# Differential attention on one Trainium2 core: the first head's split written nine units later, behind the parts of the values' third weight

## The chip, the cores and the metric

The kernel runs on one core of a Trainium2 chip. The metric is the time on the device in microseconds (us), as the median of several runs. The engines are TensorE (PE in the profile, PEld for its weight loads), VectorE (DVE), ScalarE (ACT), GpSimd (POOL) and SyncE (SP). Here SP issues the loads of weights, and POOL issues the copies between places in on-chip memory that this change moves.

## The reference

A trunk of four layers over 512 tokens of width 1024. Each layer is a mixer and a gated feed-forward block, both behind a root-mean-square norm. The mixers are S5, gated linear attention, differential attention, and S5 again. The change lies in the third layer's mixer:

```python
def diff_attn_mixer(h, positions, w_qkv, lam_q1, lam_k1, lam_q2, lam_k2, subln_g, w_o, lambda_init):
    q, k, v = jnp.split(h @ w_qkv, 3, axis=-1)
    q = partial_rope(q.reshape(bsz, seq, 2 * DIFF_HEADS, DIFF_HD), positions) * DIFF_HD ** -0.5
    k = partial_rope(k.reshape(bsz, seq, 2 * DIFF_HEADS, DIFF_HD), positions)
    v = v.astype(f32).reshape(bsz, seq, DIFF_HEADS, 2 * DIFF_HD)
    lam = (jnp.exp(jnp.sum(lam_q1 * lam_k1)) - jnp.exp(jnp.sum(lam_q2 * lam_k2)) + lambda_init)
    ...
        s = jnp.einsum('bqhd,bkhd->bhqk', qb, k)
        mask = chunk_id[:, None, None, :] <= qcid[:, None, :, None]
        p = jax.nn.softmax(jnp.where(mask, s, NEG_INF), axis=-1)
        p = p.reshape(bsz, DIFF_HEADS, 2, Q_BLOCK, seq)
        a = p[:, :, 0] - lam * p[:, :, 1]
        return jnp.einsum('bhqk,bkhd->bqhd', a, v)
    ...
    o = o * lax.rsqrt(jnp.mean(o * o, axis=-1, keepdims=True) + 1e-5) * subln_g
    o = o * (1.0 - lambda_init)
    return o.reshape(bsz, seq, D_MODEL) @ w_o
```

There are eight heads, each with two queries and two keys of 64 channels and one value of 128. A head's output is the difference of two softmaxes, applied to the values.

## The kernel before

**Precision by parts.** A float32 operand of a large matmul is split in two: a high part, which ACT makes by a cast (`high`, L346), and a low part, the remainder, which DVE makes by a subtraction (`low`, L350). A product is then three matmuls: high by high, high by low, low by high (`mm3`, lines 370 to 372). The method `last` keeps the newest instruction of each kind: `self.last["high"]` is the newest cast of a weight and `self.last["low"]` the newest remainder.

**Weights.** A weight arrives in blocks of 256 rows by 512 columns, 512 KB. SP loads a block into one of three staging buffers (`staged`, L336, tag `wst`); the parts go to one of five buffers of the tag `whl`. A buffer is claimed anew when its earlier tenant has been read for the last time.

**Units.** `gemm_units` multiplies the 512 tokens by 512 columns of a weight as a generator. Over the 1024 rows of the weight it takes four blocks in turn; a block has two slices of 128 rows, and each slice meets four tiles of 128 tokens. One unit is one slice and one tile, that is, one `mm3`; a block makes eight units and a projection 32. The block's load and split are written when its first unit is asked for. At the last slice each tile is evacuated.

**Projections.** `project(hf, z)` does this for half `hf` of the heads, with z = 0 for the queries, 1 for the keys, 2 for the values. For queries and keys the evacuation scales by the norm's factor (ACT, L2143), applies the rotation on DVE (lines 2148 to 2154), and puts the transposition of the tile into a list that is worked off six units later (`turn`: four transposes on PE, L2159, and a copy on ACT, L2160). So the keys' four tiles are turned within the first units of the values. The values are evacuated on ACT (L2165).

**The head's split.** `prepare(j)` readies head j for its scores. It casts the head's queries and keys (ACT, L2179), takes the remainder (DVE, L2180), both into a tile `hl`, and copies the parts by eight DMAs on POOL's queue (L2187 and L2188) into `qs` and `ks`, so that high and low parts lie in the two halves of the partitions. `hl` has one buffer of its own for most heads, `qs` has two, and `ks` claims one of the five buffers `whl` that the weights use too. For head 1, `hl` also claims a `whl` buffer. `scores(i)` multiplies them (PE, L2205) for tile i mod 4 of head i div 4.

**Order.** PE's instructions run in the order in which they are written. Those of the other engines, and the claims of buffers, are put in order by the compiler's scheduler, which prefers what is written first among what is ready in its own model of the time. `issue_after(x)` adds, to each instruction written in its block on the engine of x, an edge that keeps it behind x in that engine's order. It adds no semaphore.

**The sequence at the change.** Queries of the first four heads, the tables, keys, then eight units of the values; the list of turns is emptied; head 0 is prepared; the values' other 24 units follow. Then the projections of the other four heads begin, and after two of their units come the scores of head 0's first tile. The attention loop over 32 tiles runs on between the remaining units, with `prepare(j + 1)` at each head's first tile.

## Time and profile before

| | |
|---|---|
| median of 3 runs | 2325.21 us (2324.91 to 2325.57) |
| the profiled execution | 2320.61 us |
| its span, from the first to the last instruction | 2318.9 us |
| mean granted clock of TensorE | 0.989 |
| PE busy from 1250 to 1290 us | 38.51 of 40.00 us |
| PE busy from 1380 to 1440 us | 53.79 of 60.00 us |

The profile shows one execution. Busy time is summed per engine; matmuls are pipelined, so that a matmul's own length overlaps the next one's start, and the distance of two starts says more than a length. In a row of the order of time the columns are the start and the length in us, the engine, the line, the operation, output and inputs with their shapes, a count, and in brackets the idle time of that engine just before and what ended it. A row with a count above one merges neighbours. The queries' projection ends and the keys' begins near 1199.6 us of the span; the attention ends near 1460 us.

### The profile page before, as it was taken

The page shows a single profiled execution, that of the slowest core. Times are in us where ns is not written, and L with a number is a line of the kernel's source. Part 1 is how long each engine was busy: PE and PEld are TensorE (multiplying, and loading weights), DVE is VectorE, ACT ScalarE, POOL GpSimd, SP SyncE. Part 2 cuts the span into 40 slices and gives each one's busy share as a digit, 9 for nine tenths or more (in the row PEclk, how much of TensorE's full clock was granted, in tenths as well). Part 3 has the DMA queues.
Part 4 walks back from the last instruction along what each step waited for, and adds up shares of the span by engine and source line. Part 5 has one row for each costly group of instructions (what it writes and reads, how often), then busy time and mean ns, then how long its engine had stood idle before and what let it go on. Part 6 is the DMA issues. An engine that isn't in the chain of part 4 may idle for free. (4 is left out here: it accounts for less than half of the span.)

```text
span 2318.9 us, 37158 instructions
## 1 busy us (share of the span) xinstructions
PE 2221.3 (96%) x14847; PEld 1969.5 (85%) x14847; DVE 1593.3 (69%) x2461; ACT 1112.6 (48%) x1769; POOL 284.5 (12%) x394
## 2 busy tenths in 40 slices
PE   5899999999999999999999999999999899999997
PEld 3788979898877789898988887899999788989996
DVE  8784877786624578776744675976766965967674
ACT  5533645454453355555535675654534224635342
POOL 1000141522000010101002131110000100101000
PEclk8999999999999999999999999999999999999999
DMA  4156567663422457575336365876641555766531
GB/s 85 37 141 171 138 166 183 169 175 97 129 73 73 133 138 196 155 191 156 100 124 151 91 150 143 216 206 152 171 96 46 140 158 151 191 161 161 160 81 64
DMA packets 293927, 319.91 MB, mean 138 GB/s; under 512 B 70077, under 2 KB 233177, under 8 KB 293498
## 3 DMA queue, kind: packets, MB, share of 16 engines
q1 hardware_dynamic: 231130, 235.79, 33.9%
q0 software_dynamic: 62624, 81.75, 19.1%
q8 instruction: 117, 1.92, 0.3%
q14 instruction: 56, 0.46, 0.1%
HBM read 285.62 MB, written 16.65 MB: 130 GB/s over the span
## 5 line engine op out<-in xcount | busy, mean ns | idle before, releaser
L350 DVE TENSOR_TENSOR whl<-wst,whl 128x1024 fp32r<-128x1024 f32 x272 | 331.9, 1223 | 280.6 <-ACT whl L346 279.8
L346 ACT CAST whl<-wst 128x1024 fp32r<-128x1024 f32 x272 | 285.6, 1052 | 382.8 <-PE acc L372 259.8
L535 PE MATMUL a<-side,whl 128*128 128x256 f32 x3168 | 384.9, 278 | 10.0 <-ACT whl L346 5.9
L535 PEld LDWEIGHTS a<-side,whl 128*128 128x128 f32 x3168 | 371.7, 189 | 12.5 <-ACT whl L346 7.2
L370 PE MATMUL acc<-whl,act 128*128 128x512 f32 x704 | 278.0, 395 | 1.2 <-DVE g L580 0.8
L371 PE MATMUL acc<-whl,act 128*128 128x512 f32 x704 | 274.9, 391 | 0.0
L372 PE MATMUL acc<-whl,act 128*128 128x512 f32 x704 | 274.7, 390 | 0.0
L535 PE MATMUL c<-side,whl 128*128 128x256 f32 x2112 | 255.6, 277 | 5.8 <-DVE whl L350 5.8
L535 PEld LDWEIGHTS c<-side,whl 128*128 128x128 f32 x2112 | 248.1, 189 | 6.6 <-DVE whl L350 6.6
L350 DVE TENSOR_TENSOR whl<-slot,whl 128x1024 fp32r<-128x1024 f32 x105 | 127.9, 1223 | 65.7 <-ACT whl L346 65.1
L370 PEld LDWEIGHTS acc<-whl,act 128*128 128x128 f32 x704 | 132.1, 188 | 30.8 <-DVE g L580 1.2
L372 PEld LDWEIGHTS acc<-whl,act 128*128 128x128 f32 x704 | 132.2, 188 | 27.8
L371 PEld LDWEIGHTS acc<-whl,act 128*128 128x128 f32 x704 | 132.2, 188 | 26.0 <-issue 0.2
L346 ACT CAST whl<-slot 128x1024 fp32r<-128x1024 f32 x105 | 110.1, 1054 | 73.9 <-PE acc L372 28.1
L370 PE MATMUL acc<-whl,hT 128*128 128x512 f32 x352 | 142.9, 406 | 2.1 <-DVE ro L2151 1.5
L371 PE MATMUL acc<-whl,hT 128*128 128x512 f32 x352 | 137.9, 392 | 1.0 <-DVE whl L350 1.0
L372 PE MATMUL acc<-whl,hT 128*128 128x512 f32 x352 | 137.9, 392 | 0.0
L535 PE MATMUL a<-sides,whl 128*128 128x256 f32 x1056 | 134.0, 283 | 1.6 <-DVE x L518 1.6
L535 PE MATMUL d<-sides,whl 128*128 128x256 f32 x1056 | 133.4, 283 | 1.3 <-ACT whl L346 1.3
L535 PEld LDWEIGHTS a<-sides,whl 128*128 128x128 f32 x1056 | 129.5, 191 | 2.7 <-issue 2.0
L535 PEld LDWEIGHTS d<-sides,whl 128*128 128x128 f32 x1056 | 128.9, 191 | 1.9 <-ACT whl L346 1.9
L571 POOL DMA_DIRECT2D wst<-in_ffn_w_gate_up_dram x44 | 57.1, 1297 | 436.5 <-DMA wst<-in_ffn_w_gate_up_dram 239.1
(449 smaller groups left out, 3909.1 us busy)
## 6 DMA issues: line engine op xcount, KB each, us to landing
wst<-in_ffn_w_gate_up_dram SPq DMA_DIRECT2D x88, 512.0 KB, 4.7
wst<-in_ffn_w_down_dram SPq DMA_DIRECT2D x88, 512.0 KB, 4.5
slot<-in_ffn_w_gate_up_dram SPq DMA_DIRECT2D x69, 512.0 KB, 5.5
wst<-in_ffn_w_gate_up_dram POOLq DMA_DIRECT2D x44, 512.0 KB, 6.2
halves<-in_ffn_w_gate_up_dram SPq DMA_DIRECT2D x42, 512.0 KB, 5.7
wst<-in_s_w_glu_dram SPq DMA_DIRECT2D x32, 512.0 KB, 4.5
wst<-in_gla_w_in_dram SPq DMA_DIRECT2D x24, 512.0 KB, 3.7
wst<-in_diff_w_qkv_dram SPq DMA_DIRECT2D x24, 512.0 KB, 3.7
```

What stands on the lines that cost most here:

```text
L346: self.last["high"] = self.nc.scalar.copy(hl[:, 0], w[:])
L350: self.last["low"] = self.nc.vector.tensor_tensor(hl[:, 1], w[:], hl[:, 0].bitcast(F32), op=ALU.subtract)
L370: mm(out, lh, rh, start=first, stop=False)
L371: mm(out, lh, rl, start=False, stop=False)
L372: self.last["mm"] = mm(out, ll, rh, start=False, stop=last)
L535: mm(o, hl[:, x, k, c], side[:, y, k], start=first and not (j or k or n), stop=k == 3 and n == 2, skip_group_check=True,)
L571: nc.gpsimd.dma_start(w[:], left.quarter(*plus, b), accum_op=ALU.add)
```

## The change

The call `prepare(0)` is written after 17 units of the values in place of 8, and its instructions on ACT and DVE get an edge behind the newest weight's cast and remainder. With 17 units asked for, the newest weight is the values' third block (its first unit is the seventeenth). The copies on POOL's queue get no edge. What `prepare` does is unchanged, and so are PE's instructions and their order.

```diff
@@ -2273,7 +2273,9 @@
             units = project(0, 2)
             run(units, 8)
             rest()
-            prepare(0)
+            run(units, 9)
+            with self.tc.issue_after(self.last["high"].ins), self.tc.issue_after(self.last["low"].ins):
+                prepare(0)
             run(units)
 
             def projections():
```

## The prediction

> **What bounds the kernel now.** I read the page first, then the busy time by stage around the edited lines, then each engine's order of time there. The page's second line and two of its groups:

> ```profile
> span 2318.9 us, 37158 instructions
> PE 2221.3 (96%) x14847; PEld 1969.5 (85%) x14847; DVE 1593.3 (69%) x2461; ACT 1112.6 (48%) x1769; POOL 284.5 (12%) x394
> ...
> L350 DVE TENSOR_TENSOR whl<-wst,whl 128x1024 fp32r<-128x1024 f32 x272 | 331.9, 1223 | 280.6 <-ACT whl L346 279.8
> L346 ACT CAST whl<-wst 128x1024 fp32r<-128x1024 f32 x272 | 285.6, 1052 | 382.8 <-PE acc L372 259.8
> ```

> The matmul engine is busy for 96%: an edit on another engine is worth what it removes of PE's waits, no more. A weight's two parts cost 1.05 us on ACT (the cast, L346) and 1.22 us on DVE (the remainder, L350), and ACT mostly waits for PE (L372) to give back a buffer. By stage:

> ```profile
> 1176.00:1223.00 47.00, 47.00 (x221) 38.95 (x220) 16.30 (x42) 14.15 (x21) 1.88 (x2) 1.00 0.38 130
> 1223.00:1250.00 27.00, 25.43 (x119) 20.55 (x118) 11.69 (x21) 14.00 (x19) 6.40 (x12) 1.00 0.71 164
> ```

> The columns are length, then PE, weight loads, DVE, ACT, POOL, granted clock, DMA share, GB/s. The queries' and keys' projections (first row) have no idle PE; the values' (second row) has 1.57 us of it, 27.00 - 25.43, and that is where the moved call stands. PE in order of time:

> ```profile
> 1230.07 0.40 PE L371 MATMUL acc<-whl,hT 128*128 128x512 f32 x1
> 1230.30 0.40 PE L372 MATMUL acc<-whl,hT 128*128 128x512 f32 x1
> 1231.31 0.50 PE L370 MATMUL acc<-whl,hT 128*128 128x512 f32 x1 [0.61 <-ACT whl L346]
> 1232.76 0.50 PE L371 MATMUL acc<-whl,hT 128*128 128x512 f32 x1 [0.96 <-DVE whl L350]
> 1233.10 0.39 PE L372 MATMUL acc<-whl,hT 128*128 128x512 f32 x1
> 1233.33 0.39 PE L370 MATMUL acc<-whl,hT 128*128 128x512 f32 x1
> ...
> 1250.36 1.07 PE L2205 MATMUL s<-ks,qs 128*128 128x512 f32 x4
> ```

> Matmuls start 0.23 us apart, except at one unit: it first waits for a cast, then for a remainder. That is unit 8, the first of the second weight: the last row, head 0's scores, comes after the values' 32 units and two more, and counting back from 1250.36 by 0.68 us a unit gives 25 units to 1233.3, so 1233.33 is unit 9. From 1230.30 to 1233.33 are 3.03 us for four starts, against 4 x 0.227 = 0.91. **The stall costs 2.12 us**, refill of the pipeline included. Now ACT and DVE over the same time:

> ```profile
> 1188.93 1.06 ACT L346 CAST whl<-wst 128x1024 fp32r<-128x1024 f32 x1 [4.37 <-PE acc L372]
> 1194.38 1.06 ACT L346 CAST whl<-wst 128x1024 fp32r<-128x1024 f32 x1 [4.38 <-PE acc L372]
> ...
> 1200.40 1.04 ACT L346 CAST whl<-wst 128x1024 fp32r<-128x1024 f32 x1
> ...
> 1203.88 0.59 ACT L2160 COPY qk<-qTp 128x512 f32<-128x512 f32 x1 [0.55 <-PE qTp L2159]
> 1205.02 0.59 ACT L2160 COPY qk<-qTp 128x512 f32<-128x512 f32 x1 [0.55 <-PE qTp L2159]
> 1221.43 2.73 ACT L2143 ACTIVATE qtm<-acc,rcol 128x512 f32<-128x512 f32 x4 [15.83 <-PE acc L372]
> ...
> 1228.64 0.59 ACT L2160 COPY qk<-qTp 128x512 f32<-128x512 f32 x1 [0.55 <-PE qTp L2159]
> 1229.26 1.05 ACT L2179 CAST hl<-qk 128x1024 fp32r<-128x1024 f32 x1
> 1230.22 2.94 ACT L346 CAST whl<-wst 128x1024 fp32r<-128x1024 f32 x3
> ...
> 1245.48 2.00 ACT L2179 CAST hl<-qk 128x1024 fp32r<-128x1024 f32 x2 [2.00 <-DMA ks<-hl]
> ```

> ```profile
> 1222.15 0.29 DVE L2148 TENSOR_TENSOR ro<-acc,cos2r 128x128 f32<-128x128 f32 x1 [19.25 <-ACT qtm L2143]
> ...
> 1230.35 1.23 DVE L2180 TENSOR_TENSOR hl<-qk,hl 128x1024 fp32r<-128x1024 f32 x1 [5.00 <-ACT hl L2179]
> 1231.49 3.49 DVE L350 TENSOR_TENSOR whl<-wst,whl 128x1024 fp32r<-128x1024 f32 x3
> ```

> Until 1200 a weight is cast every 5.5 us (1188.93, 1194.38), which is eight units: the prefetch runs a full weight ahead. Then no cast comes for thirty microseconds, though ACT stands idle for 15.83 and DVE for 19.25, and three come at once behind the head's split (hl). They were not waiting for data, as the loads show:

> ```profile
> 1184.11 18.99 SPq L336 DMA_DIRECT2D wst<-in_diff_w_qkv_dram  x5
> ...
> 1232.74 2.64 SPq L336 DMA_DIRECT2D wst<-in_diff_w_qkv_dram  x3
> ```

> The last load before the gap is issued near 1202.7, and no staging buffer comes free until 1232.74, so three weights lie staged. Nor was PE slow: it ate the keys' weights steadily. What is left is the buffer claims. The code has five buffers of tag whl, and ks of head 0 takes one; it is written ahead of the values' second weight, so I read the gap as that weight's claim standing behind the claim of ks, which waits for the split, which waits for the last transposed keys (1228.64 + 0.59 = 1229.23).

> **The change part by part.** No instruction is added or removed. One ACT cast, one DVE subtraction, eight DMA issues on POOL and the claims of hl, qs, ks, st and o_s are written nine units later, and the cast and subtraction get an edge behind the third weight's cast and remainder.

> *What moves ahead.* The second weight claims the buffer of the keys' first weight. The keys' units begin 23.6 us before the values' (32 x 0.682, and four transposed tiles of about 0.45, since the copies behind them come 1.14 apart, 1203.88 and 1205.02, where a unit takes 0.68), the values' at 1230.53 - 8 x 0.682 - 1.8 = 1223.3; so that buffer is free at about 1199.7 + 7.3 = 1207.0 and the next at 1212.4. Both casts and both remainders (1.05 + 1.22 us each) then lie in the idle stretch that the rows above show, beside PE's matmuls. Unit 8 needs them at 1230.53: some 16 us of cover. Gain: the whole 2.12 us. The bounds: none of it, if the casts stay where they are; 2.12, if both parts are early. I take 2.12, since the steady rows before 1200 are the nearest to the new order.

> *What moves back.* The edge costs nothing if the third weight's parts are done at about 1214.7: the split then starts when its keys are there, at 1229.26 as now. The fourth weight now stands behind the claim of ks, with its cast at 1230.22 and remainder from 1231.6 to 1232.8; PE needs it at unit 24, 1230.53 + 16 x 0.682 = 1241.4, a cover of 8.6 us. If that cover went, it would cost what the second weight costs now, 2.12. Were the edge itself to wait, this cast and remainder are what stands behind it on ACT and DVE, and PE would wait for them.

> *The eight DMAs and the queue they share.* POOL issues them behind the split:

> ```profile
> 1230.62 1.13 POOL L2187 DMA_DIRECT2D qs<-hl  x2 [47.14 <-ACT hl L2179]
> ...
> 1235.16 0.63 POOL L2188 DMA_DIRECT2D ks<-hl  x1
> ...
> DMA to landing us min/median/max: 3.3/4.8/10.1
> ```

> POOL has nothing else to do there (47.14 us idle), so nothing queues behind them. The last row is that of ks from 1225 to 1262: up to 10.1 us to land. ACT's next split waits for these copies until 1245.48, so they need 1245.48 - 1229.26 = 16.2 us from the cast. Scores of head 0, now at 1250.36, would come at 1248.24: the cover shrinks from 4.9 to 2.8 us but holds. SP's three loads of 1232.74 partly move ahead, to about 1209 and 1215, when the remainders free the staging; two follow-on loads take their place beside the copies. From none of these to all moved, the landing changes by no more than the spread of that row, 3.3 to 10.1; I take the present one. [...]

> *Sum and later stages.* The profiled execution took 2320.61 us, 1.7 outside its span; less 2.12 this is 2318.49. It lies 4.60 under the median of the runs, 2325.21, so the forecast for the median is **2323.1**. For the gain to last, what comes later must start from PE. It does where the chain leaves PE for longest:

> ```profile
> 1513.76 2.37 DVE whl L350 x2
> 1516.15 13.22 DMA halves<-in_ffn_w_gate_up_dram
> ```

> This load, the longest piece of transfer in the chain behind the attention, begins when a remainder frees its buffer, and so shifts with it. Between stand some short waits of PE, whose order of DVE and ACT work may come out differently:

> ```profile
> PE acc L370 <- ACT oT L488: 2.4, 2, 1.7
> PE op L2237 <- ACT aT L2229: 1.7, 4, 0.7
> PE acc L370 <- DVE ro L2151: 1.5, 1, 1.5
> PE op L2237 <- ACT qk L2160: 1.2, 1, 1.2
> ```

> **The rivals.** *Queue order, not claims.* If the casts stay behind the keys' copies on ACT and only swap with the split, the second weight is cast at 1229.26 to 1230.31 and its remainder ends at 1231.58 (the split's own rows). The cast is in time for 1230.53; the second matmul, due at 1230.76, waits 0.9, with 0.1 of refill: 1.0 lost, 1.1 won, **2324.1**. For it: three casts sit together on ACT. Against it: the steady casts before. [...]

> *Slower: the head's copies land late.* The edge only says that the split may not come before the third weight. If ACT's order puts it behind the next weight casts as well, up to that which needs the values' second weight eaten (1230.53 + 8 x 0.682 = 1236.0, and 1.05 for the cast), the split starts at 1237.0, lands at 1253.2, and PE waits 5.0 at the scores: 2325.21 - 2.12 + 5.0 = **2328.1**. It decides from a split 2.8 us later than now, and costs one for one from there; 9.6 us later it is 2329.9. Against it: those casts are written behind the split and nothing holds it to them.

> *Given back.* The waits listed last grow by what was won, because the splits of later heads wait for DMAs (2.00 us at 1245.48) whose landing need not follow PE: **2325.2**. For it: that wait. Against it: the copies are issued behind PE's scores.

> *More than the stall.* The waits on ro and qk, 1.5 and 1.2 us of the same attention loop, go too as ACT's and DVE's orders shift: 2323.1 - 2.7 = **2320.4**. For it: both are cases of a short operation queued behind others. Against it: nothing in the edit touches them.

> **How the numbers follow.** Forecast 0.49, queue order 0.13, late copies 0.17, given back 0.10, more 0.11. This kernel's measurement tells about 0.2%, 4.65 us, from no change, so faster begins below 2320.56 and slower above 2329.86. Only the last rival lies below, 0.11; of the late copies I put 0.10 beyond 2329.86, since a split held further, behind the values' evacuations, would cost more than the case priced; 0.79 remains. The likeliest case's own range is 2321.4 to 2324.8: the four short waits, 6.8 us together, moving by a quarter. The range for 8 in 10 reaches to the rival with more, 2320.4, and part of the way to late copies, **2320.2 to 2327.2**.

> **What would show it.** Right: two weight casts between 1205 and 1221; no wait of PE at unit 8; the split still starting within 0.2 us of the last keys' copy; head 0's scores 2.1 us earlier, and the same shift at the end of the attention. Wrong: casts still bunched behind the copies (queue order); a wait of L2205 on ks (late copies); the shift present at the scores and gone at the output projection (given back). A change beyond 4.65 us would mean that the order of the attention loop, and not this stall, decides.

## The result, and the profile after

| | before | after |
|---|---|---|
| median beside each other | 2326.74 us (2324.91 to 2332.58, 9 runs) | 2320.83 us (2316.11 to 2323.99, 9 runs) |
| ratio, 95% interval | | 0.9972 (0.9962 to 0.9983) |
| the profiled execution | 2320.61 us | 2322.66 us |
| its span, mean granted clock | 2318.9 us, 0.989 | 2320.9 us, 0.984 |

The kernel became 0.28% faster, with the interval reaching from 0.17% to 0.38%. The forecast was 2323.1 us, 2.1 below the median then known; the medians now lie 5.9 apart. The time lies at the low end of the range given, and below the likeliest case's own range. The one profile of after is longer than the one of before, so single executions can't be compared by their spans here.

From the page of after:

```profile
span 2320.9 us, 37157 instructions
...
PE 2226.6 (96%) x14847; PEld 1975.5 (85%) x14847; DVE 1593.6 (69%) x2461; ACT 1111.1 (48%) x1769; POOL 284.2 (12%) x394
...
L350 DVE TENSOR_TENSOR whl<-wst,whl 128x1024 fp32r<-128x1024 f32 x272 | 332.0, 1223 | 289.3 <-ACT whl L346 288.3
L346 ACT CAST whl<-wst 128x1024 fp32r<-128x1024 f32 x272 | 285.3, 1051 | 385.0 <-PE acc L372 269.8
```

Counts and durations are those of before. The busy time by stage, in the same columns as before (length, PE, weight loads, DVE, ACT, POOL, clock, DMA share, GB/s):

```profile
1176.00:1223.00 47.00, 47.00 (x222) 38.94 (x221) 21.18 (x44) 16.84 (x26) 1.86 (x2) 1.00 0.44 153
1223.00:1250.00 27.00, 27.00 (x128) 22.39 (x127) 8.90 (x21) 10.96 (x14) 6.65 (x12) 1.00 0.64 125
```

In the second row PE's 1.57 us of idle time are gone, and the first has the ACT and DVE work that moved ahead (16.84 and 21.18, from 14.15 and 16.30). The rows are cut at fixed times, and this execution runs 4.3 us later than that of before up to here, so they don't hold quite the same work. ACT of after in order of time:

```profile
1204.73 1.04 ACT L346 CAST whl<-wst 128x1024 fp32r<-128x1024 f32 x1
...
1211.42 1.05 ACT L346 CAST whl<-wst 128x1024 fp32r<-128x1024 f32 x1 [1.50 <-PE acc L372]
1216.86 1.05 ACT L346 CAST whl<-wst 128x1024 fp32r<-128x1024 f32 x1 [4.39 <-PE acc L372]
1225.75 2.73 ACT L2143 ACTIVATE qtm<-acc,rcol 128x512 f32<-128x512 f32 x4 [7.83 <-PE acc L372]
...
1232.97 0.59 ACT L2160 COPY qk<-qTp 128x512 f32<-128x512 f32 x1 [0.55 <-PE qTp L2159]
1233.59 1.05 ACT L2179 CAST hl<-qk 128x1024 fp32r<-128x1024 f32 x1
1234.55 2.00 ACT L346 CAST whl<-wst 128x1024 fp32r<-128x1024 f32 x2
...
1249.18 1.05 ACT L2179 CAST hl<-qk 128x1024 fp32r<-128x1024 f32 x1 [2.19 <-DMA ks<-hl]
1250.14 2.42 ACT L2165 ACTIVATE vall<-acc,rcol 128x512 f32<-128x512 f32 x4
```

Two casts lie at 1211.42 and 1216.86, in what was a gap of 15.83 us, each released by PE giving back a buffer. The split follows the last turned keys by 0.03 us (1232.97 + 0.59 against 1233.59), the fourth weight's cast follows it, and the last two rows are head 2's split, which waits for head 0's copies, and the values' evacuations behind it. The waits of PE in after from 1250 to 1460 us (total, times, longest):

```profile
PE acc L370 <- ACT oT L488: 2.3, 2, 1.7
PE op L2237 <- ACT aT L2229: 1.8, 4, 0.7
PE acc L370 <- DVE ro L2151: 1.3, 1, 1.3
PE op L2237 <- ACT qk L2160: 1.2, 1, 1.2
```

All four short waits are still there at nearly their sizes in this execution.

### The profile page after: what moved, and what is told of

Read it like the earlier page. It is cut to its first block, busy times and chain, and to the rows that moved or that the text cites. A ratio compares the mean times of both kernels' runs of the same rounds, so it can differ in the third digit from the quotient of the medians.

```text
span 2320.9 us, 37157 instructions
## 1 busy us (share of the span) xinstructions
PE 2226.6 (96%) x14847; PEld 1975.5 (85%) x14847; DVE 1593.6 (69%) x2461; ACT 1111.1 (48%) x1769; POOL 284.2 (12%) x394
## 5 line engine op out<-in xcount | busy, mean ns | idle before, releaser
L350 DVE TENSOR_TENSOR whl<-wst,whl 128x1024 fp32r<-128x1024 f32 x272 | 332.0, 1223 | 289.3 <-ACT whl L346 288.3
L346 ACT CAST whl<-wst 128x1024 fp32r<-128x1024 f32 x272 | 285.3, 1051 | 385.0 <-PE acc L372 269.8
L370 PE MATMUL acc<-whl,act 128*128 128x512 f32 x704 | 278.8, 396 | 1.1 <-DVE g L580 1.0
L371 PE MATMUL acc<-whl,act 128*128 128x512 f32 x704 | 275.5, 391 | 0.0
L372 PE MATMUL acc<-whl,act 128*128 128x512 f32 x704 | 275.4, 391 | 0.0
L350 DVE TENSOR_TENSOR whl<-slot,whl 128x1024 fp32r<-128x1024 f32 x105 | 127.8, 1222 | 66.3 <-ACT whl L346 66.2
L370 PEld LDWEIGHTS acc<-whl,act 128*128 128x128 f32 x704 | 132.5, 188 | 31.1 <-DVE g L580 2.1
L372 PEld LDWEIGHTS acc<-whl,act 128*128 128x128 f32 x704 | 132.5, 188 | 28.0
L371 PEld LDWEIGHTS acc<-whl,act 128*128 128x128 f32 x704 | 132.6, 188 | 26.2 <-issue 0.2
L346 ACT CAST whl<-slot 128x1024 fp32r<-128x1024 f32 x105 | 110.0, 1052 | 73.9 <-PE acc L372 28.1
L370 PE MATMUL acc<-whl,hT 128*128 128x512 f32 x352 | 142.7, 405 | 1.3 <-DVE ro L2151 1.3
L372 PE MATMUL acc<-whl,hT 128*128 128x512 f32 x352 | 138.2, 393 | 0.0
L371 PE MATMUL acc<-whl,hT 128*128 128x512 f32 x352 | 137.8, 392 | 0.0
```

What stands on the lines that cost most here:

```text
L346: self.last["high"] = self.nc.scalar.copy(hl[:, 0], w[:])
L350: self.last["low"] = self.nc.vector.tensor_tensor(hl[:, 1], w[:], hl[:, 0].bitcast(F32), op=ALU.subtract)
L370: mm(out, lh, rh, start=first, stop=False)
L371: mm(out, lh, rl, start=False, stop=False)
L372: self.last["mm"] = mm(out, ll, rh, start=False, stop=last)
```

## The experiments

**How executions are compared.** All kernels have the same 14847 matmuls in the same order. So the time between two fixed matmuls can be taken in every trace, and the first profile's subtracted. A stretch runs from one fixed matmul to another, each the first to start after the time that names it in before's first profile, and a minus is time won. The diffs of this section are against the changed kernel, and lines that only keep an instruction for later are left out.

```
kernel                       1228-1236  1236-1250  1250-1270  1270-1300 us
before, first profile           0.00       0.00       0.00       0.00
e1_before_again                +1.60       0.00       0.00      +1.28
e5_before_look2                +1.58       0.00       0.00      +0.66
e6_before_look3                -0.01       0.00      -0.01      +0.48
e7_before_look4                +1.59      +0.02       0.00      +1.45
after, first profile           -2.15       0.00      -0.01      -0.21
e2_after_again                 -2.15       0.00      -0.01      -0.65
e9_after_look3                 -2.15       0.00       0.00      -0.91
e10_after_look4                -2.15       0.00       0.00      +0.20
e3_one_unit                    -2.15      +0.77      +0.01      +0.03
e4_ks_late                     -2.15      +1.04       0.00      -0.07
e8_split_held                  -2.15      +4.51     +11.36      +0.65
e11_cast_behind_copies         -1.24      +6.40      +1.53      +0.48
e12_fourth_weight              -2.15       0.00      -0.01      -0.52
```

**Both kernels again.** e1, e5, e6 and e7 are the kernel before, unedited; e2, e9 and e10 the changed one. e1, e2, e3, e4 and e12 were timed in twelve executions each, beside the kernel before; the others are one execution each.

> The kernel before, unchanged, timed against itself. Theory A (the change wins the 2.1 us stall and the rest of the measured 5.9 us between the medians is scatter of executions): the ratio is 1.000 within 0.0015, and single executions differ by several us, as the TensorE clock is granted at half speed in a varying number of short spells. Theory B (the change wins some 6 us for good): the ratio is 1.000 within 0.0005 and executions lie within 2 us.

> The changed kernel once more. Theory A: ratio 0.9991, that is 2.1 us, with an interval that holds 0.9991. Theory B: ratio 0.997 to 0.9975 again and an interval that leaves 0.9991 out. In the order of time both expect no wait of the matmul engine at the values' unit 8.

e1 took 2325.63 us, ratio 0.9992 (0.9979 to 1.0005); e2 2322.68, ratio 0.9979 (0.9968 to 0.9990). So before doesn't differ from itself by more than the interval allows, and the gain repeats, at 4.0 us between medians. Neither theory fits whole: 2.1 us, a ratio of 0.9991, lies just outside e2's interval, and e2 came back smaller than the 5.9 us that theory B took for lasting; the twelve executions of e1 lie 12 us apart, not 2. The trace of e1 has something that the first profile of before lacks. Its matmuls at the stall:

```profile
1231.93 0.40 PE L372 MATMUL acc<-whl,hT 128*128 128x512 f32 x1
1232.94 0.51 PE L370 MATMUL acc<-whl,hT 128*128 128x512 f32 x1 [0.61 <-ACT whl L346]
1234.40 0.50 PE L371 MATMUL acc<-whl,hT 128*128 128x512 f32 x1 [0.95 <-DVE whl L350]
...
1236.15 0.63 PE L370 MATMUL acc<-whl,hT 128*128 128x512 f32 x1
1236.58 0.63 PE L371 MATMUL acc<-whl,hT 128*128 128x512 f32 x1
...
1238.85 0.40 PE L371 MATMUL acc<-whl,hT 128*128 128x512 f32 x1
1239.08 0.39 PE L372 MATMUL acc<-whl,hT 128*128 128x512 f32 x1
```

The stall is the same, 0.61 and 0.95 us. Behind it the starts are 0.43 us apart (1236.15 to 1236.58) in place of 0.23, until 1238.6. The granted clock says why (columns as above, the clock third from the end):

```profile
1230.00:1236.00 6.00, 4.44 (x18) 3.08 (x17) 4.02 (x4) 4.48 (x5) 3.13 (x6) 0.92 0.39 72
1236.00:1242.00 6.00, 6.00 (x22) 4.81 (x22) 1.84 (x2) 1.05 (x1) 1.41 (x3) 0.79 1.26 279
```

The clock was halved for 3.41 us, from 1235.1, and this costs 1.60 us more, which no row of waits shows. Three more profiles of before and two more of after show how often.

> The kernel before, for its profile alone. Theory C (the stall at unit 8 is sometimes followed by a spell of half clock, which adds 1.6 us to it, so the change wins 2.1 in some executions and 3.7 in others): the granted clock between 1225 and 1245 us of the span falls below 1.00 in more than half of such profiles, and the stretch from the last matmul of unit 7 to unit 16 is 1.6 us longer where it does. Theory A (2.1 us and scatter elsewhere): the spell of the earlier profile was a chance, and the stretch is that of the first profile.

> As the run before: theory C expects the spell behind the stall in more than half of these profiles, theory A in none.

> As the two runs before: theory C expects the spell behind the stall in more than half of these profiles, theory A in none.

> The changed kernel, for its profile. Theory C: no stall at unit 8 and so no spell of half clock between 1225 and 1245 us; the stretch from unit 7 to unit 16 is 2.15 us shorter than in the first profile of before, to 0.05. The wait of ACT for head 2's copies to land, before its split of head 3, is under 3.0 us as in the two profiles so far (before: 3.15 to 4.61). Theory A: the same stretch, and that wait anywhere between 2.4 and 4.6.

> As the run before: no spell, 2.15 us shorter, and by theory C a wait of ACT for head 2's copies under 3.0 us.

They took 2329.73, 2322.51 and 2328.93 us before, 2320.10 and 2329.12 after. In the table's first column before has about +1.6 in three of five executions and 0 in two; after has -2.15 in all four. So the stall cost 2.15 us or 3.75, in the mean of the five 0.95 + 2.15 = 3.1 us, and the change removes both parts. Why e10 is long nevertheless is told under scatter, below.

The last column was also expected to differ, by ACT's wait ahead of head 3's split, and this came out in part. In e1 and in e2:

```profile
1283.05 1.05 ACT L2179 CAST hl<-qk 128x1024 fp32r<-128x1024 f32 x1 [4.42 <-DMA ks<-hl]
```

```profile
1280.19 1.05 ACT L2179 CAST hl<-qk 128x1024 fp32r<-128x1024 f32 x1 [2.48 <-DMA ks<-hl]
```

Over the nine executions of the two kernels this wait and the last column go together one for one: 3.15, 3.60, 3.81, 4.42 and 4.61 us before, with 0, 0.48, 0.66, 1.28 and 1.45; 2.22, 2.48, 2.90 and 3.36 after, with -0.91, -0.65, -0.21 and +0.20. What PE loses there is thus ACT's wait for head 2's copies. Its mean falls from 3.92 to 2.74, 1.2 us, but the two sets overlap (3.15 before, 3.36 in e10, where less than 3.0 was expected). PE's own waits there say where it shows. PE waits on aT (L2229) for 0.3, 0.5, 1.1 and 1.3 us in e6, e5, e1 and e7; the first profile of before and the four of after list no such wait. On ro (L2151) it waits for 1.5 us in all five of before, and for 0.7, 0.9, 1.3 and 1.5 in after. On qk it is 1.2 in all nine.

**One weight ahead, or three.** e3 writes the split after 9 units of the values, e12 after 25.

```diff
-            run(units, 9)
+            run(units, 1)
```

> The split written one unit later, behind the second weight's parts alone. If the claim of ks is what holds the later weights back: one weight cast early (near 1207 us of the span), the third and fourth bunched behind the split, which is early enough, so the stall is gone all the same and the time is that of the changed kernel, 2.1 us under before in the aligned traces. If two weights have to be early: a wait of about 1 us or more of the matmul engine at unit 16.

```diff
-            run(units, 9)
+            run(units, 17)
```

> The split written after 25 units, behind the fourth weight's parts. Three weight casts come early and none is left behind the claim of ks. No more is to be won at unit 8, so the same time as the changed kernel, ratio 0.998 to before, within 0.0015. If the loads that now start still earlier change where head 2's copies land, it shows in the stretch from 1270 to 1300 us, by up to 1 us either way.

e3 took 2323.56 us, ratio 0.9982 (0.9970 to 0.9994); e12 2322.70, 0.9978 (0.9965 to 0.9991). In both, unit 8's stall is gone, since the second weight alone is what that unit lacks; e12's last column, -0.52, lies among those of after. But e3 has a new wait. Its PE and its ACT:

```profile
1249.40 0.50 PE L370 MATMUL acc<-whl,hT 128*128 128x512 f32 x1 [0.48 <-ACT vall L2165]
```

```profile
1231.17 1.05 ACT L2179 CAST hl<-qk 128x1024 fp32r<-128x1024 f32 x1
1232.12 2.94 ACT L346 CAST whl<-wst 128x1024 fp32r<-128x1024 f32 x3
...
1247.71 1.05 ACT L2179 CAST hl<-qk 128x1024 fp32r<-128x1024 f32 x1 [3.14 <-DMA ks<-hl]
1248.66 2.41 ACT L2165 ACTIVATE vall<-acc,rcol 128x512 f32<-128x512 f32 x4
```

In e12, ACT:

```profile
1230.18 1.05 ACT L2179 CAST hl<-qk 128x1024 fp32r<-128x1024 f32 x1
...
1243.84 1.05 ACT L2179 CAST hl<-qk 128x1024 fp32r<-128x1024 f32 x1 [0.26 <-DMA ks<-hl]
1245.93 2.73 ACT L2165 ACTIVATE vall<-acc,rcol 128x512 f32<-128x512 f32 x4 [1.04 <-PE acc L372]
```

On ACT, head 2's split stands ahead of the values' evacuations (L2165), and the next projection's first unit needs an accumulator that these empty. Head 2's split waits for head 0's copies. In e3 it came 16.5 us after head 0's split, and the evacuations were 0.48 us late for PE; in e12 it came 13.7 us after, and they waited for PE. That PE matmul starts 0.25 to 0.73 us after the first evacuation ends in the four executions of after, 1.15 us after it in e12, and 0.05 us where PE waits for it: the changed kernel has only 0.2 to 0.7 us to spare there. In the five executions of before the same matmul starts 0.53 to 1.15 us after it, so the change took some of this slack.

**Claim or order.** e4 writes head 0's cast, remainder and four copies into `qs` after eight units, as before, and only the claim of `ks` with its four copies (here a function `copies`) after 17.

```diff
             rest()
+            prepare(0)
             run(units, 9)
-            with self.tc.issue_after(self.last["high"].ins), self.tc.issue_after(self.last["low"].ins):
-                prepare(0)
+            copies(0, *first[0], False)
```

> The head's cast, subtraction and the four copies to qs stay written after 8 units; only the claim of ks and its four copies are written after 17, without any edge. If the claim of ks held the weights back: two weight casts between 1205 and 1221 us, no wait at unit 8, the same time as the changed kernel. If the order of the casts on ACT held them back: three casts bunched behind the split, the stall of 2.1 us is there and the time is that of before.

It took 2322.39 us, ratio 0.9982 (0.9968 to 0.9996). Unit 8's stall is gone as with the whole change (-2.15), though the split is written where it was and has no edge. Its ACT has the two early casts, in an execution that is 7.9 us late ahead of the edit:

```profile
1214.99 1.05 ACT L346 CAST whl<-wst 128x1024 fp32r<-128x1024 f32 x1 [1.50 <-PE acc L372]
1220.43 1.05 ACT L346 CAST whl<-wst 128x1024 fp32r<-128x1024 f32 x1 [4.38 <-PE acc L372]
```

It was the claim of `ks`, moved here with nothing but the four copies into it, that held the weights. The time is not quite that of after in the trace: its 1.04 us in the second column holds a wait of 0.75 at the evacuations, as in e3.

**The split held for long.** In e8 head 0 is prepared after all 32 units, behind the first evacuation of the values (kept as `last["value"]` at L2165).

```diff
-            run(units, 9)
-            with self.tc.issue_after(self.last["high"].ins), self.tc.issue_after(self.last["low"].ins):
-                prepare(0)
             run(units)
+            with self.tc.issue_after(self.last.pop("value").ins):
+                prepare(0)
```

> Head 0 is prepared after all 32 units of the values, behind the first evacuation on ACT, with the claim of ks and the copies behind that. By the price in the prediction (16.2 us from the start of the split to the landed copies): the split starts near 1246 us of a span like the first profile's, the copies land near 1262, and the matmul engine waits 12 to 14 us at head 0's scores, so the time is 10 to 12 us over before. If the copies land faster with fewer loads beside them (10 us from the split): the wait is 7 to 8 us and the time 5 to 6 us over before. The stall at unit 8 is gone in both.

It took 2343.86 us. PE in its order of time:

```profile
1255.39 0.80 PE L370 MATMUL acc<-whl,hT 128*128 128x512 f32 x1 [2.35 <-ACT whl L346]
1256.65 0.80 PE L371 MATMUL acc<-whl,hT 128*128 128x512 f32 x1 [0.46 <-DVE whl L350]
...
1261.09 1.19 PE L2207 MATMUL s<-ks,qs 128*128 128x512 f32 x2 [1.94 <-issue]
...
1268.73 1.19 PE L2207 MATMUL s<-ks,qs 128*128 128x512 f32 x2 [6.45 <-DMA ks<-hl]
```

(L2207 is here the scores' line, L2205 of the others.) The split began at 1251.63. Ahead of the edit this execution is 1.7 us later than after's first profile, so the split is 16.3 us later than there, and the copies were there 17.1 us behind it. The table has 15.9 us for it in two columns, against 16.3 - 2.8 = 13.5 by the prediction's price of late copies. But only 8.4 us (1.94 + 6.45) are waits at the scores, where 12 to 14 were expected, and 2.8 (2.35 + 0.46) are a wait for the next projection's weight, which is cast only behind the split. That this is the claim of `ks` again fits e4, but no run isolates it. The other 4.7 us go by while the clock is halved, for 17 us from 1255.3, the end of the first of these waits.

**The cast behind the turned keys.** e11 keeps the change and holds the second weight's cast behind the keys' last copy, which is the rival of queue order made real (`last["turned"]` is the newest copy of L2160).

```diff
-            run(units, 9)
+            with self.tc.issue_after(self.last.pop("turned").ins):
+                run(units, 1)
+            run(units, 8)
```

> The changed kernel with the second weight's cast held behind the last of the keys' copies, so that ACT's order is copies, second weight, third weight, split. This is the rival of the queue's order built on purpose: the matmul engine's second matmul of unit 8 waits 0.9 us for the remainder, 1.0 us lost in all and so 1.1 won against the first profile of before in that stretch; the split starts 2.0 us later than in the changed kernel, and head 0's scores do not wait, since 2.8 us are covered. If a loss of 1 us is too short to bring a spell of half clock, the granted clock stays 1.00 there.

It took 2331.30 us. Its ACT and its PE:

```profile
1227.06 0.59 ACT L2160 COPY qk<-qTp 128x512 f32<-128x512 f32 x1 [0.55 <-PE qTp L2159]
1227.55 2.00 ACT L346 CAST whl<-wst 128x1024 fp32r<-128x1024 f32 x2
1229.44 1.04 ACT L2179 CAST hl<-qk 128x1024 fp32r<-128x1024 f32 x1
...
1249.72 1.04 ACT L2179 CAST hl<-qk 128x1024 fp32r<-128x1024 f32 x1 [7.74 <-DMA qs<-hl]
1250.67 2.41 ACT L2165 ACTIVATE vall<-acc,rcol 128x512 f32<-128x512 f32 x4
```

```profile
1229.90 0.50 PE L371 MATMUL acc<-whl,hT 128*128 128x512 f32 x1 [0.57 <-DVE whl L350]
1251.40 0.80 PE L370 MATMUL acc<-whl,hT 128*128 128x512 f32 x1 [5.07 <-ACT vall L2165]
```

At unit 8 it does what the rival said: the remainder is late, and of 2.15 us won 0.91 is lost (1.0 forecast). What follows was not expected. Head 2's split comes 20.3 us after head 0's, and PE waits 5.07 us for the evacuations behind it; 2.9 us more go by 1270, with the clock halved for 6.83 us from 1250.1. At unit 8 itself it stayed full. The copies themselves landed later. The loads and copies from 1225 to 1262 (count, KB each, median us to landing), in e11 and, from 1228 to 1266, in after:

```profile
wst<-in_diff_w_qkv_dram SPq DMA_DIRECT2D x5, 512.0 KB, 10.2
ks<-hl POOLq DMA_DIRECT2D x8, 256.0 KB, 8.0
qs<-hl POOLq DMA_DIRECT2D x8, 128.0 KB, 8.7
```

```profile
wst<-in_diff_w_qkv_dram SPq DMA_DIRECT2D x5, 512.0 KB, 5.1
ks<-hl POOLq DMA_DIRECT2D x8, 256.0 KB, 5.4
qs<-hl POOLq DMA_DIRECT2D x8, 128.0 KB, 3.8
```

Five loads of weights and sixteen copies in both, but in e11 all five loads are issued from just before the first copy on, and in after two of them only behind head 0's copies. That this slows both down is an argument: before, too, issues five loads beside head 0's copies, and they need 16.2 to 17.05 us there. In e11 head 1's copies also begin 7.5 us before the split that waits for head 0's (1242.27 against 1249.72), in after 1.9 us (1247.28 against 1249.18). e11 is one execution.

**Scatter between executions.** e9 and e10 are one kernel, and their spans are 9.0 us apart (2318.4 and 2327.4). 8.8 of these arise before 1200 us, ahead of the edit, as the same comparison of matmuls shows. There the instructions of all these kernels are the same. So a kernel's gain is read from the stretches behind the edit, or from many runs, and not from one span.

## Why the prediction was right, and where its size was off

**The stall and its cause: right.** The prediction's 2.12 us at unit 8 is -2.15 in every execution of the changed kernel. That the weights stood behind the claim of `ks` was an inference from the order of the text; e4 shows it.

**What moves ahead and back: right.** Casts were forecast at about 1207.0 and 1212.4; they come at 1211.42 and 1216.86 in an execution that is 4.3 us late, that is 1207.1 and 1212.5. The split starts within 0.2 us of the keys' last copy, and the fourth weight's cast behind it makes PE wait for nothing. From head 0's split to head 2's, which waits for the copies, it took 15.2 to 15.7 us in four executions, 16.2 forecast.

**The edge and the given-back gain: right.** The two edges cost nothing, and the gain is kept: the short waits stay but for part of the one on ro, and from 1300 us to the end the four executions of after differ from before's by no more than before's do among themselves.

**The size: too small, and the step is the cost of the stall.** The term "The stall costs 2.12 us" was read from one execution, in which the clock stayed full. In three of five it is 3.75, so the mean is 3.1.

Another 1.2 us comes from ACT's shorter wait for head 2's copies; that its size goes one for one into PE's time is shown, but not why it is shorter. The copies are not issued earlier: head 2's first leaves POOL at 1265.80 in the first profile of before and at 1268.25 in that of after, which is 0.3 us later against PE's matmuls (which are 2.18 us late there). They land faster: those into `ks` take 8.3 and 9.0 us from issue to landing, in the median, in before and e1, and 8.0 and 7.3 in after and e2. Head 1's copies do not start together with them in either kernel: POOL has issued the last of those 13 us earlier before the change (by 1252.61) and 14 us earlier after it (by 1254.02). The cause stays open.

Together this is 4.3 us, against 5.9 (4.0 to 8.8 by the interval) and, in e2, 4.0 (2.3 to 7.4). Up to 1.6 us more stay open, which the scatter does not let us see. The forecast's sum has neither the half clock nor this wait of ACT. That its range still holds the measured time, at the low end, is partly luck: the range reaches so far down only for the sake of "More than the stall".

**The starting point.** The forecast took 2.12 from 2325.21, the median of three runs; that of nine was 2326.74. Less 4.3 this gives 2322.4, between the two medians of the changed kernel, 2320.83 and 2322.68.

The prediction's own sign that the attention loop decides, a change beyond 4.65 us, is met by the 5.9 us of the first comparison and not by the 4.0 of e2. The traces show what of the loop moved, the 1.2 us above, and no more of it stands out.

**The rivals.** "More than the stall" named nearly the right number, 2320.4, for a reason that holds only in small part: of the waits on ro and qk, which should have gone, the first fell from 1.5 us to 1.1 in the mean of four executions, and the second stayed at 1.2. Queue order was refuted by the casts at 1211.42. Late copies did not happen, but the place where they would decide was wrong. The prediction took the scores, with 2.8 us of cover. What is late first is head 2's split on ACT and the evacuations queued behind it, with 0.2 to 0.7 us; e3 (0.48), e4 (0.75) and e11 (5.07) all pay there. The question "what is queued behind the waiting instruction on its engine" was asked for POOL and for the edge, and not for this wait of ACT. Its chance should have been higher for that reason.

## What to carry to other kernels

Where a pool of buffers is shared, a claim written early for something that is ready late can hold back the claims behind it (here for 2.15 us of PE, as e4 shows): write it where its data come, and look for a gap of casts with the inputs already staged. To size a stall, read several executions and the granted clock behind it, since what follows can cost nearly as much again (here 1.6 us behind 2.15). Before a wait is called covered, list what stands behind it on the waiting engine's own queue, and not only who reads the data.

## What the hardware showed that was not expected

A count of the grid's periods from 600 to 2290 us in the first profiles of before and after goes with this in part. Half clock follows a period of full clock twelve times: once in each near 675 us, where PE has no idle time, and ten times behind a period with 1.93 to 3.41 us of it. No other period was followed by it, and three of those had 1.57, 1.57 and 1.78 us of idle time, no less than the 1.56 of e1, e5 and e7, which were followed. What else decides there, and what happens near 675 us, is open. By the grid an estimate can be made for this stall: from the start of the first wait to the end of the second are 2.06 us, so if the stall may fall anywhere in a period, and the spell comes where both waits lie in one as in e1, e5 and e7, some 4 in 10 executions, (3.41 - 2.06) / 3.41, would have it, and the stall's mean cost would be 2.8 us in place of 3.1.

Eight copies between places in on-chip memory, 1.5 MB in all, took from 13.7 us (e12) to 20.3 us (e11) from the split's cast to the start of the split that waits for them. Beside them SP issued two loads of weights in e12, three in after (15.2 to 15.7 us), five in before (16.2 to 17.05) and five in e11. The number of loads alone doesn't set the time: before and e11 differ at the same five, and e8 took 17.1 us with two, while head 1's copies ran beside head 0's.
